# Address of one kind of weight parts in two tiles, and the grouping of 32 transposes, in a macaron layer

## Chip, cores, metric

One NeuronCore of a Trainium2 chip runs the whole kernel. The metric is the device time of one launch in microseconds; the profile is of one execution, and its span runs from the first to the last instruction.

## The reference

One layer on x of 512 tokens by 1024 channels, float32 throughout. What matters here is the feed-forward network (FFN), which is computed before and after a mixer:

```python
def swiglu_ffn(x, w_gate, w_up, w_down):
    return (jax.nn.silu(x @ w_gate) * (x @ w_up)) @ w_down

x = x + 0.5 * swiglu_ffn(rmsnorm(x, ffn1_norm[l]), ffn1_w_gate[l], ffn1_w_up[l], ffn1_w_down[l])
x = x + hybrid_mixer(rmsnorm(x, mix_norm[l]), ...)
x = x + 0.5 * swiglu_ffn(rmsnorm(x, ffn2_norm[l]), ffn2_w_gate[l], ffn2_w_up[l], ffn2_w_down[l])
x = rmsnorm(x, final_norm[l])
```

D_MODEL is 1024, D_FF is 2816, so `w_gate` and `w_up` have 22 tiles of 128 columns each. The mixer (attention over chunks and trailing means) is not touched by the change.

## The kernel before

**Products.** A float32 product is made of three float32r matmuls: each operand is split into a high part (`hi`, rounded to float32r) and a low part (`lo`, the rest), and `mm3` (lines 205 to 210) issues hi x hi (L208), hi x lo (L209) and lo x hi (L210) into one PSUM bank. ScalarE makes the high parts (a cast), VectorE the low ones (a subtraction). In the FFN's first half the weights are the stationary operand, which PE loads before each matmul, and the normalised x is the moving one.

**`ffn_up`** computes gate and up of one FFN (`loaded` is false in the first, true in the second). The 22 pairs of weight tiles are taken in two ways. The first `plain` = 5 pairs are multiplied directly: 8 row blocks of x, moving operand 512 tokens wide. The other 17 pairs, n = 5 to 21, go through a Strassen-like scheme with seven products of half size in place of eight: x's blocks are combined once into A11, A12, A22, S1 to S4, each 256 tokens wide, and per pair the weights' blocks are used as they are or added up. These are the half-size tiles. Each makes four sets of parts, `w[n, 11]` (W1), `w[n, 13]` (W1+W3 and a like sum), `w[n, 24]` (two longer sums) and `w[n, 22]` (helpers `high11` to `low24`, lines 520 to 580), and seven products of 12 matmuls of 256 columns, in this order: `w11` with A11; the second half of `w13` with S3; the first of `w24` with S2 and its second with A22; the first half of `w13` with S1; two with `w22`. So the second and the fifth product read the parts `w[n, 13]`.

**Where parts lie.** `part_tiles` hands out pairs of SBUF buffers of `ROOM` = 1152 elements in a cycle of four, so that each kind of parts always gets buffers of the same kind; `w[n, 13]` always gets the pair in the FFN's own pool. A part takes 1024 elements, from element `at` of its buffer: `AHEAD_OF_PARTS` = 16 for the half-size tiles. A buffer begins at 384 mod 512 bytes, so a part at element 16 begins at 448 mod 512 and one at element 32 (`OFF_AT`) at 0 mod 512. `high13` uses `OFF_AT` where `n - plain` is in `OFF`.

**The opening of the second FFN.** Here PE, VectorE and ScalarE run in the order in which the code is recorded. `OPENING` (line 63) writes it out by hand, token by token: `Wi` splits the i-th weight block into `w[i]` and fetches block i + 3; `B0` to `B3` multiply the first two pairs of tiles, two row blocks at a time, into the four banks `first` (24 triples of matmuls in all B1 to B3; `B3` is `last_block`); `P` and `L` are the tiles behind; `g`, `u`, `m` evacuate; `p` takes a piece of the work that combines x's blocks. B1 and B2 are `block(w, kp)` with kp 1 and 2: for each of two row blocks kk, four triples, one to each bank. Among these triples stand 32 transposes, `further`, one `by_token` each (line 1659): a 128x128 block of x, copied by DMA into the float32r tiles `xr` (rows 0 to 3 in the first, 4 to 7 in the second), is transposed on PE (L1666) into a PSUM bank of the four with tag "a". After every fourth one ScalarE copies the bank into a temporary (L1671) and SyncE's queue stores it to `x_d` in device memory (L1672), from where it is read again in the FFN's second half. The same queue issues the weight loads (L187, L522), in an order that a scheduler sets.

Of the kernel before, what the change touches and what calls it, by code (L numbers as in the profile page):

```python
# [21 lines left out]
NT = S // P  # L22
# [15 lines left out]


ROOM, AHEAD_OF_PARTS, ALIGN = 1024 + 128, 16, 64  # L40
OFF, OFF_AT = (0, 2, 6), 32
PLAIN = (5, 5)
RATES = [[2] * (n - 1) + [0] + [2] * (FF // P - n - 2) + [0] * 2 for n in PLAIN]
PROBS = 3
# [31 lines left out]
def layer(  # L76
# [51 lines left out]
    def temp(dtype=F32):  # L128
        return tpool.tile([P, S], dtype, tag="t", name=name("t"))

    def bank(tag="mm", bufs=4):
        return ps.tile([P, S], F32, tag=tag, name=name(tag), bufs=bufs)
# [52 lines left out]
    def raw_of(src):  # L185
        raw = raw_tile()
        nc.sync.dma_start(raw, src)  # L187
        return raw

    def parts_of(raw):  # L190
        hi, lo = part_tiles()
        split(raw, hi, lo)
        return hi, lo
# [11 lines left out]
    def mm3(acc, a, b, start, stop, further=False):  # L205

        more = dict(skip_group_check=True) if further else {}
        nc.tensor.matmul(acc, a[0], b[0], start=start, stop=False, **more)  # L208
        nc.tensor.matmul(acc, a[0], b[1], start=False, stop=False, **more)  # L209
        nc.tensor.matmul(acc, a[1], b[0], start=False, stop=stop, **more)  # L210

    def cut(pair, lo, n):
        if isinstance(pair[0], list):
            pair, lo = [z[lo // S] for z in pair], lo % S
        return pair[0][:, lo : lo + n], pair[1][:, lo : lo + n]
# [233 lines left out]
    def ffn_up(norm, wA, down, loaded, parts=(), aside=(), further=()):  # L449
# [24 lines left out]
        def block(w, kp):  # L474
            for kk in range(2):
                k = 2 * kp + kk
                for j in range(4):
                    mm3(first[j], cut(w, (kk * 4 + j) * P, P), norm.h[k], k == 0, k == KD - 1)
                    if kp:
                        for _ in range(min(1 + (j == 3), len(further))):  # L480
                            further.pop(0)()

        def nothing():
            pass
# [10 lines left out]
        def read_in():  # L495
            for kp in range(KD // 2):
                load(2 * kp)
                w = weights(wA[kp], 1 if kp else 4)
                load(2 * kp + 1)
                norm.square(2 * kp)  # L500
                norm.square(2 * kp + 1)
                if kp == KD // 2 - 1:
                    with tc.high_priority():
                        norm.finish(AF.Silu)
                block(w, kp)
            for f in range(2):
                sg = evacuate(f, *first[2 * f : 2 * f + 2])
                down.make_sums(sg, 2)
            blocks_of()
# [3 lines left out]
        def fetch(n, which):  # L513

            if n < KF:
                f = down.order[n]
                raw = raws[n, which] = down.pool.tile(
                    [P, 2 * S], F32, tag=which, name=name("raw"), bufs=RAW
                )
                half = slice(0, S) if which == "ra" else slice(S, 2 * S)  # L520
                for i, j in enumerate((1, 0) if which == "ra" else (0, 1)):
                    nc.sync.dma_start(raw[:, i * S : (i + 1) * S], wA[2 * f + j][:, half])  # L522
# [14 lines left out]
        def high11(n):  # L537
            if n < KF:
                high(n, (n, 11), raws[n, "ra"][:, :S])

        def low11(n):
            if n < KF:
                low((n, 11))

        def sum13(n):
            if n < KF:
                z = w[n, "odd"] = new_sum()
                a, b = raws[n, "ra"], raws[n, "rb"]
                nc.vector.tensor_tensor(z[:, :S], a[:, :S], a[:, S:], op=ALU.add)
                nc.vector.tensor_tensor(z[:, S:], a[:, S:], b[:, :S], op=ALU.add)  # L550

        def sum24(n):
            if n < KF:
                z = w[n, "even"] = new_sum()
                raw, odd = raws[n, "rb"], w[n, "odd"]
                nc.vector.tensor_tensor(z[:, :S], odd[:, :S], raw[:, :S], op=ALU.add)
                nc.vector.tensor_tensor(z[:, S:], z[:, :S], raw[:, S:], op=ALU.add)

        def high13(n):
            if n < KF:  # L560
                off = n - plain in OFF
                high(n, (n, 13), w[n, "odd"], OFF_AT if off else AHEAD_OF_PARTS)

        def low13(n):
            if n < KF:
                low((n, 13))

        def high24(n):
            if n < KF:
                high(n, (n, 24), w[n, "even"])  # L570

        def low24(n):
            if n < KF:
                low((n, 24))

        def opening():

            banks, halves_of = {f: first[2 * f : 2 * f + 2] for f in range(2)}, {}
            raw = dict(enumerate(parts[1:], 1))
            w = {0: parts[0]}  # L580
            steps = norm.steps()

            def fetch_raw(i):
                if i < 2 * plain and i not in raw:
                    raw[i] = raw_of(wA[i])

            def prepare(i):
                w[i] = parts_of(raw[i])
                fetch_raw(i + 3)

            def last_block():
                for j in range(4):
                    for kk in range(2):
                        k = KD - 2 + kk
                        mm3(first[j], cut(w[3], (kk * 4 + j) * P, P), norm.h[k], False, k == KD - 1)
                        for _ in range(min(1 + kk, len(further))):
                            further.pop(0)()

            def tile_product(n, j):
                acc = bank()  # L600
                banks.setdefault(n, []).append(acc)
                for k in range(KD):
                    mm3(acc, cut(w[2 * n + j], k * P, P), norm.h[k], k == 0, k == KD - 1)

            def last_tile(part):
                n = plain - 1
                if part == 0:
                    banks[n] = [bank(), bank()]
                for k in range(2 * part, 2 * part + 2):
                    for j in range(2):  # L610
                        mm3(
                            banks[n][j], cut(w[2 * n + j], k * P, P), norm.h[k], k == 0, k == KD - 1
                        )

            def gate(f):
                g, sg = temp(), temp()
                nc.vector.tensor_tensor(g, banks[f][0], norm.rb, op=ALU.mult)
                nc.scalar.activation(sg, g, AF.Silu)
                halves_of[f] = sg

            def up(f):
                sg = halves_of[f]
                nc.vector.tensor_tensor(sg, sg, norm.rb, op=ALU.mult)
                down.place(f, banks[f][1], sg)

            def sums(f):
                down.sums(f)
                down.make_sums(halves_of[f], 2)

            def half_size(what):  # L630
                n = plain
                if what == 0:
                    high11(n)
                    low11(n)
                elif what == 1:
                    sum13(n)
                elif what == 2:
                    high13(n)
                    low13(n)
                elif what == 3:  # L640
                    sum24(n)
                elif what == 4:
                    high24(n)
                else:
                    low24(n)

            def loads(what):
                fetch(plain + what // 2, ("ra", "rb")[what % 2])

            do = {  # L650
                "W": prepare, "B": lambda i: block(w[i], i) if i < 3 else last_block(),
                "P": lambda i: tile_product(i // 10, i % 10), "L": last_tile, "g": gate, "u": up,
                "m": sums, "h": half_size, "F": loads, "n": lambda i: next(steps), "p": piece,
                "O": lambda i: down.open(range(1, G - 3) if i else range(G - 3, G)),
            }
            for token in OPENING.split():
                do[token[0]](int(token[1:] or 1))
            assert not todo and not further
            return partial(up, plain - 1), partial(sums, plain - 1)
# [1241 lines left out]
```

## Time and profile before

| | |
|---|---|
| median of 3 runs | 837.81 us (837.65 to 838.47) |
| profiled execution | 838.23 us, span 836.5 us |
| PE busy | 826.8 us, 99% of the span |
| VectorE, ScalarE busy | 712.0 us (85%), 501.8 us (60%) |
| share of PE in the chain that ended last | 97% |
| half-size tiles | 62.4 to 224.7 us and 560.5 to 722.8 us |
| B1 to B3 of the second FFN | 507.8 to 527.8 us |

In PE's timeline a row's first number is the start of a matmul. Its length is modelled and overlaps the next one's, so what a matmul costs is read from one start to the next.

### The profile page before, as it was taken

The numbers are of one execution on the slowest core, as the hardware profiler recorded it, in microseconds if no ns is written. First come the engines' busy times: TensorE is split into PE (matmuls) and PEld (weight loads), VectorE is DVE, ScalarE is ACT, GpSimd is POOL, SyncE is SP. The second block draws the span as 40 slices with busy tenths as digits, with TensorE's granted clock in tenths as the row PEclk, the third lists the DMA queues.
The fourth block names the chain that finished last, engine by engine and source line by source line (L and its number), as shares of the span: only waits on it lengthen the run. The fifth ranks groups of instructions, "written<-read, shape, count | busy, mean of one in ns | idle before, by whom it ended". The sixth has DMA issues, their size and how long they took to land.

```text
span 836.5 us, 14350 instructions
## 1 busy us (share of the span) xinstructions
PE 826.8 (99%) x5288; PEld 740.3 (89%) x5288; DVE 712.0 (85%) x1157; ACT 501.8 (60%) x859; POOL 150.0 (18%) x212
## 2 busy tenths in 40 slices
PE   9999999999999999999999999999999999999996
PEld 7889999999988888887888887889999999988885
DVE  7999998899897678766979668989889999887896
ACT  8446555665675656558747745455566555756573
POOL 0312211222074000102111000111221121132600
PEclk9999999999999999999999999999999999999999
DMA  8667788888689973332221137757877888689922
GB/s 300 183 198 170 200 210 243 201 207 207 193 245 271 329 233 110 108 110 89 76 69 62 67 110 263 235 154 216 215 212 217 214 204 211 228 269 340 323 87 101
DMA packets 78839, 160.63 MB, mean 192 GB/s; under 512 B 7328, under 2 KB 30384, under 8 KB 78384
## 3 DMA queue, kind: packets, MB, share of 16 engines
q1 hardware_dynamic: 55680, 113.03, 40.1%
q0 software_dynamic: 22656, 46.14, 26.0%
q8 instruction: 41, 0.67, 0.3%
q10 hardware_dynamic: 432, 0.54, 0.2%
q14 instruction: 30, 0.25, 0.1%
HBM read 153.38 MB, written 50.34 MB: 244 GB/s over the span
## 4 chain that ended last, share of the span: by engine, by line
PE 97%; DMA 1%; DVE 1%; ACT 0%; SPq 0%; issue 0%; DVEq 0%
PE mm L208 23%; PE mm L210 23%; PE mm L209 23%; PE a L208 8%; PE a L209 8%; PE a L210 8%; PE a L1438 1%; PE a L1374 1%; PE a L1426 1%; DMA x<-in_xT_dram 1%; PE a L1296 0%; PE a L1666 0%; PE a L327 0%; PE a L1029 0%; PE mm L1029 0%; SPq L201 0%
## 5 line engine op out<-in xcount | busy, mean ns | idle before, releaser
L155 DVE TENSOR_TENSOR wlo<-raw,whi 128x1024 fp32r<-128x1024 f32 (+2 forms) x115 | 124.4, 1088 | 25.9 <-ACT whi L154 25.3
L154 ACT CAST whi<-raw 128x1024 fp32r<-128x1024 f32 (+2 forms) x115 | 107.3, 944 | 49.2 <-PE mm L210 13.0
L209 PE MATMUL mm<-ha,whi 128*128 128x256 f32 x408 | 112.8, 276 | 0.0
L208 PE MATMUL mm<-ha,whi 128*128 128x256 f32 x408 | 112.8, 276 | 0.0
L210 PE MATMUL mm<-ha,wlo 128*128 128x256 f32 x408 | 112.7, 276 | 0.0
L721 ACT ACTIVATE t<-mm 128x256 f32<-128x256 f32 x102 | 39.2, 384 | 114.3 <-PE mm L210 111.6
L531 DVE TENSOR_TENSOR wlo<-wsum,whi 128x1024 fp32r<-128x1024 f32 x68 | 83.0, 1220 | 11.0 <-PE mm L210 7.9
L866 POOL COPY mark<-t 128x1 f32<-128x1 f32 x44 | 14.3, 324 | 391.6 <-DVE t L774 243.0
L208 PE MATMUL mm<-hhi,whi 128*128 128x512 f32 x192 | 76.6, 401 | 0.9 <-ACT whi L154 0.6
L209 PEld LDWEIGHTS mm<-ha,whi 128*128 128x128 f32 x408 | 76.6, 188 | 0.1
L208 PEld LDWEIGHTS mm<-ha,whi 128*128 128x128 f32 x408 | 76.6, 188 | 0.1
L210 PEld LDWEIGHTS mm<-ha,wlo 128*128 128x128 f32 x408 | 76.6, 188 | 0.0
L209 PE MATMUL mm<-hlo,whi 128*128 128x512 f32 x192 | 74.9, 391 | 0.0
L210 PE MATMUL mm<-hhi,wlo 128*128 128x512 f32 x192 | 74.8, 391 | 0.0
L868 POOL DMA_DIRECT2D wsum<-in_wB_dram x72 | 71.1, 1102 | 12.3 <-issue 7.5
L526 ACT CAST whi<-wsum 128x1024 fp32r<-128x1024 f32 x68 | 67.9, 1047 | 2.0 <-PE mm L209 1.5
L209 PE MATMUL mm<-wlo,ah 128*128 128x512 f32 x176 | 68.5, 389 | 0.0
L210 PE MATMUL mm<-whi,ah 128*128 128x512 f32 x176 | 68.5, 389 | 0.0
L208 PE MATMUL mm<-whi,ah 128*128 128x512 f32 x176 | 68.4, 389 | 0.0
L531 DVE TENSOR_TENSOR wlo<-raw,whi 128x512 fp32r<-128x512 f32 x68 | 62.0, 950 | 0.0
L526 ACT CAST whi<-raw 128x512 fp32r<-128x512 f32 x68 | 56.2, 827 | 2.5 <-issue 2.5
L208 PE MATMUL a<-whi,ah 128*128 128x512 f32 (+1 forms) x154 | 55.7, 362 | 0.0
(233 smaller groups left out, 2398.7 us busy)
## 6 DMA issues: line engine op xcount, KB each, us to landing
raw<-in_wA_dram SPq DMA_DIRECT2D x136, 256.0 KB, 4.1
wsum<-in_wB_dram POOLq DMA_DIRECT2D x60, 512.0 KB, 6.9
raw<-wsum SPq DMA_DIRECT2D x40, 512.0 KB, 4.8
raw<-in_wB_dram SPq DMA_DIRECT2D x30, 512.0 KB, 7.4
wsum<-wsum POOLq DMA_DIRECT2D x20, 512.0 KB, 5.2
raw<-in_wA_dram SPq DMA_DIRECT2D x19, 512.0 KB, 4.1
x<-in_xT_dram SPq DMA_DIRECT2D x16, 256.0 KB, 8.8
raw<-in_wQK_dram SPq DMA_DIRECT2D x8, 512.0 KB, 3.5
```

The costliest lines, as they stand in the source:

```text
L154: nc.scalar.copy(hi, src)
L155: nc.vector.tensor_tensor(lo, src, hi.bitcast(F32), op=ALU.subtract)
L208: nc.tensor.matmul(acc, a[0], b[0], start=start, stop=False, **more)
L209: nc.tensor.matmul(acc, a[0], b[1], start=False, stop=False, **more)
L210: nc.tensor.matmul(acc, a[1], b[0], start=False, stop=stop, **more)
L526: nc.scalar.copy(hi, src)
L531: nc.vector.tensor_tensor(lo, src, hi.bitcast(F32), op=ALU.subtract)
L721: nc.scalar.activation(dst, src, AF.Copy, scale=scale)
L866: nc.gpsimd.tensor_copy(mark, after[:, 0:1])
L868: nc.gpsimd.dma_start(self.rows(i, g), self.rows(self.terms[i][at], g), **(dict(accum_op=ALU.add) if at else {}),)
L1374: nc.tensor.matmul(banks[i][:, at : at + n], qT[pair][0][a][rows, t * P : (t + 1) * P], kT[pair][0][b][rows, :n], start=a + b == 0, stop=a ...
L1426: nc.tensor.transpose(tp[:, n : n + P], prob[h, t][:, j * P : (j + 1) * P], ident)
```

## The change

`OFF` keeps its first entry alone, so that in the third and seventh half-size tile of both FFNs (n - plain = 2 and 6) W1+W3's parts begin at element 16 as in the others; the tiles' first entry keeps them at element 32. The transposes are no longer recorded behind each triple of B1, B2 and B3, but in runs of eight behind each of the two row blocks of B1 and of B2; B3 has none.

```diff
-OFF, OFF_AT = (0, 2, 6), 32
+OFF, OFF_AT = (0,), 32
...
                 for j in range(4):
                     mm3(first[j], cut(w, (kk * 4 + j) * P, P), norm.h[k], k == 0, k == KD - 1)
-                    if kp:
-                        for _ in range(min(1 + (j == 3), len(further))):
-                            further.pop(0)()
+                for _ in range(min(2 * NT if kp else 0, len(further))):
+                    further.pop(0)()
...
                         mm3(first[j], cut(w[3], (kk * 4 + j) * P, P), norm.h[k], False, k == KD - 1)
-                        for _ in range(min(1 + kk, len(further))):
-                            further.pop(0)()
```

The first edit moves no instruction, only addresses. The second moves instructions on PE, ScalarE and SyncE's queue; from L480 on, lines of the kernel after stand one to three lower in number.

PE at the end of B1's first row block, before. `mm_6068`, `mm_6069` and `mm_6066` are banks of `first`, `whi_6074` and `wlo_6075` are B1's weights, `a_6131` and `a_6148` the banks of the first and second four transposes:

```order
L210 MATMUL mm_6068<-hhi_5953,wlo_6075 128x512
L1666 MATMUL a_6131<-ident_r,xr_6049 128x128
L208 MATMUL mm_6069<-hhi_5953,whi_6074 128x512
L209 MATMUL mm_6069<-hlo_5954,whi_6074 128x512
L210 MATMUL mm_6069<-hhi_5953,wlo_6075 128x512
L1666 MATMUL a_6131<-ident_r,xr_6049 128x128
L1666 MATMUL a_6148<-ident_r,xr_6049 128x128
L208 MATMUL mm_6066<-hhi_5963,whi_6074 128x512
L209 MATMUL mm_6066<-hlo_5964,whi_6074 128x512
```

PE at the same place, after (`a_6140` and `a_6148` are the first two banks here):

```order
L208 MATMUL mm_6069<-hhi_5953,whi_6074 128x512
L209 MATMUL mm_6069<-hlo_5954,whi_6074 128x512
L210 MATMUL mm_6069<-hhi_5953,wlo_6075 128x512
L1663 MATMUL a_6140<-ident_r,xr_6049 128x128 x4
L1663 MATMUL a_6148<-ident_r,xr_6049 128x128 x4
L208 MATMUL mm_6066<-hhi_5963,whi_6074 128x512
L209 MATMUL mm_6066<-hlo_5964,whi_6074 128x512
L210 MATMUL mm_6066<-hhi_5963,wlo_6075 128x512
```

The transposes that stood singly behind each triple now follow one another in two groups of four, and the fourth triple of the row block follows the third directly.

ScalarE from the first copy out of a transposes' bank to the second SiLU, before. `whi_6171` is W3's high part (read in B3) and `whi_6229` W4's (read by P20); the rows L618 are the SiLU of the first two gates, the `a_` names are the banks of four transposes each:

```order
L1671 COPY t_6145<-a_6131 128x512
L1671 COPY t_6162<-a_6148 128x512
L154 CAST whi_6171<-raw_6056 128x1024
L1671 COPY t_6186<-a_6168 128x512
L1671 COPY t_6203<-a_6192 128x512
L1671 COPY t_6220<-a_6209 128x512
L154 CAST whi_6229<-raw_6078 128x1024
L1671 COPY t_6250<-a_6239 128x512
L1671 COPY t_6267<-a_6256 128x512
L1671 COPY t_6281<-a_6270 128x512
L618 ACTIVATE t_6285<-t_6284 128x512
L618 ACTIVATE t_6290<-t_6289 128x512
```

The same, after (`whi_6184` is W3's, `whi_6253` is W4's):

```order
L1668 COPY t_6145<-a_6140 128x512
L1668 COPY t_6153<-a_6148 128x512
L1668 COPY t_6173<-a_6168 128x512
L1668 COPY t_6181<-a_6176 128x512
L154 CAST whi_6184<-raw_6056 128x1024
L1668 COPY t_6208<-a_6203 128x512
L1668 COPY t_6216<-a_6211 128x512
L1668 COPY t_6236<-a_6231 128x512
L1668 COPY t_6244<-a_6239 128x512
L154 CAST whi_6253<-raw_6078 128x1024
L615 ACTIVATE t_6285<-t_6284 128x512
L615 ACTIVATE t_6290<-t_6289 128x512
```

Four copies now stand ahead of W3's cast where there were two, and eight ahead of W4's where there were five; none stands between W4's cast and the SiLU.

SyncE's queue, before: `x_d` rows are stores of transposed x, `raw_6233` is the load for W7, `raw_6175` that for W6, `raw_6482` the first loads of the half-size tiles:

```order
L1672 DMA x_d<-t_6145 128x512
L187 DMA raw_6233<-in_wA_dram 128x1024
L1672 DMA x_d<-t_6162 128x512
L187 DMA raw_6175<-in_wA_dram 128x1024
L1672 DMA x_d<-t_6186 128x512
L187 DMA raw_6327<-in_wA_dram 128x1024
L1672 DMA x_d<-t_6203 128x512
L522 DMA raw_6482<-in_wA_dram 128x512
L1672 DMA x_d<-t_6220 128x512
L522 DMA raw_6482<-in_wA_dram 128x512
```

After (`raw_6188` for W6, `raw_6257` for W7):

```order
L1669 DMA x_d<-t_6145 128x512
L1669 DMA x_d<-t_6153 128x512
L187 DMA raw_6188<-in_wA_dram 128x1024
L1669 DMA x_d<-t_6173 128x512
L1669 DMA x_d<-t_6181 128x512
L187 DMA raw_6257<-in_wA_dram 128x1024
L1669 DMA x_d<-t_6208 128x512
L1669 DMA x_d<-t_6216 128x512
L187 DMA raw_6327<-in_wA_dram 128x1024
L1669 DMA x_d<-t_6236 128x512
L1669 DMA x_d<-t_6244 128x512
L521 DMA raw_6482<-in_wA_dram 128x512 x2
```

W6's and W7's loads stand behind the second and the fourth store, where the first and the second of the two stood behind the first and the second store; the loads of the half-size tiles stand behind all eight.

## The prediction

> **What bounds the kernel now.** I read the page first: busy times, the granted clock, then the chain of work that ended last.
>
> ```profile
> span 836.5 us, 14350 instructions
> PE 826.8 (99%) x5288; PEld 740.3 (89%) x5288; DVE 712.0 (85%) x1157; ACT 501.8 (60%) x859; POOL 150.0 (18%) x212
> PEclk9999999999999999999999999999999999999999
> PE 97%; DMA 1%; DVE 1%; ACT 0%; SPq 0%; issue 0%; DVEq 0%
> L531 DVE TENSOR_TENSOR wlo<-wsum,whi 128x1024 fp32r<-128x1024 f32 x68 | 83.0, 1220 | 11.0 <-PE mm L210 7.9 <-ACT whi L526 2.7
> ```
>
> TensorE is the chain (97%), at the full granted clock throughout. VectorE, which makes the low parts of the weights, mostly waits for TensorE where it is idle ahead of the 1024-wide subtraction (7.9 of 11.0 us). So a change counts by what it does to the distances between starts of matmuls on PE, provided that no operand comes late. Both edits act there, and I read both from starts in PE's timeline.
>
> **The parts' place, third and seventh half-size tile.** A half-size tile is 7 products of 12 matmuls. Its second and fifth product load W1+W3's parts as the stationary operand; these are the only instructions on PE that the first edit touches. In the first FFN the third such tile starts at 81.64 and the fourth at 91.28. PE's timeline, with the first matmul of the first, second and third product of each:
>
> ```profile
> 81.64 0.28 PE L208 MATMUL mm<-ha,whi 128*128 128x256 f32 x1
> ...
> 83.00 0.28 PE L208 MATMUL a<-xa,whi 128*128 128x256 f32 x1
> ...
> 84.42 0.28 PE L208 MATMUL mm<-xa,whi 128*128 128x256 f32 x1
> ...
> 91.28 0.28 PE L208 MATMUL mm<-ha,whi 128*128 128x256 f32 x1
> ...
> 92.64 0.28 PE L208 MATMUL a<-xa,whi 128*128 128x256 f32 x1
> ...
> 94.00 0.28 PE L208 MATMUL mm<-xa,whi 128*128 128x256 f32 x1
> ```
>
> The second product takes 1.42 us in the third tile (parts at 0 mod 512 bytes), 1.36 us in the fourth (parts 64 bytes before such a place). The first product, whose parts are never moved, takes 1.36 us in both. Whole tiles, by windows from one tile's first matmul to the next (third, fourth, seventh, eighth; first FFN, then second):
>
> ```profile
> 81.64:91.28 9.64, 9.64 (x87) 1.00 0.81 247
> 91.28:100.80 9.52, 9.52 (x87) 1.00 0.82 210
> 119.84:129.48 9.64, 9.64 (x87) 1.00 1.03 217
> 129.48:139.00 9.52, 9.52 (x87) 1.00 0.90 224
> 579.73:589.37 9.64, 9.64 (x86) 1.00 0.82 265
> 589.37:598.89 9.52, 9.52 (x86) 1.00 0.79 208
> 617.93:627.57 9.64, 9.64 (x86) 1.00 0.98 218
> 627.57:637.09 9.52, 9.52 (x86) 1.00 0.81 221
> ```
>
> Four tiles are 0.12 us longer than their neighbours. With the parts at the ordinary place I take 9.52 us for them: 4 x 0.12 = **0.48 us saved**. Is VectorE ready for that? Its idle time waits for PE, so its work moves forward with PE. Zero is one bound (the tile would be slow for another reason); the other bound is a loss, the rival "slow pace" below.
>
> **The transposes.** 32 transposes of x, 128 columns each, stand among the 72 matmuls of 512 columns of B1, B2 and B3 in the second FFN. Before, one or two follow each group of three matmuls: 16 single, 8 pairs. After, eight follow each half of B1 and of B2, none stands in B3. PE's timeline around a single and a pair, then the last pair and the undisturbed matmuls behind it:
>
> ```profile
> 510.15 0.22 PE L1666 MATMUL a<-ident_r,xr 128*128 128x128 f32 x1
> 510.21 0.45 PE L208 MATMUL mm<-hhi,whi 128*128 128x512 f32 x1
> ...
> 510.96 0.28 PE L1666 MATMUL a<-ident_r,xr 128*128 128x128 f32 x2
> 511.08 0.46 PE L208 MATMUL mm<-hhi,whi 128*128 128x512 f32 x1
> ...
> 511.84 0.22 PE L1666 MATMUL a<-ident_r,xr 128*128 128x128 f32 x1
> ...
> 527.80 0.46 PE L208 MATMUL mm<-hhi,whi 128*128 128x512 f32 x1
> 528.10 0.39 PE L209 MATMUL mm<-hlo,whi 128*128 128x512 f32 x1
> ...
> 528.78 0.39 PE L209 MATMUL mm<-hlo,whi 128*128 128x512 f32 x1
> ```
>
> Three undisturbed matmuls take 0.68 us (528.10 to 528.78). With a single transpose the group takes 510.96 - 510.15 = 0.81, with a pair 511.84 - 510.96 = 0.88. So a single costs 0.13 us and the second of a pair 0.07. Over the whole stretch, from B1's first matmul at 507.84 to the first behind the last pair:
>
> ```profile
> 507.84:527.80 19.96, 19.96 (x106) 1.00 0.69 228
> ```
>
> 24 groups would take 24 x 0.68 = 16.32, so the transposes cost 19.96 - 16.32 = 3.64; the matmul at 527.80 holds the next back for 0.30 instead of 0.23, so 3.71 in all. With 24 x 0.13 = 3.12 for the first of each place, 8 seconds have 0.59, 0.07 each; rounding of 0.01 us in each start lets it be 0.07 to 0.09. I take 0.08. A run of eight then costs 0.13 + 7 x 0.08 = 0.69, and some 0.02 more because matmuls behind an interruption settle over more than the three that now follow. Four runs: 4 x 0.71 = 2.84. **Saved: 3.71 - 2.84 = 0.87 us.**
>
> The price of the third to eighth transpose of a run is not in the trace. Below it lies 0.06 (the two starts of the pair at 510.96 are followed by the next matmul's at 511.08): a run then costs 0.57, four 2.28, saved 1.43. Above it lies the kernel's longest run of transposes, ten of plain float32 in the mixer:
>
> ```profile
> 422.03 1.25 PE L1426 MATMUL a<-ident,prob 128*128 128x128 f32 x10
> 423.04 0.48 PE L208 MATMUL mm<-hhi,whi 128*128 128x512 f32 x1
> 423.35 0.40 PE L209 MATMUL mm<-hlo,whi 128*128 128x512 f32 x1
> ```
>
> From 422.03 to 423.35 are ten transposes and one matmul of 0.23: 1.09, or 0.11 each. By that a run of eight costs 0.13 + 7 x 0.11 + 0.02 = 0.92, four 3.68: saved 0.03. I take 0.08, since the pair is the same instruction on the same tiles. A loss would need PE to wait inside or before a run. A run fills two of the four "a" banks, and ScalarE empties a bank in 0.59 us (below) while 12 matmuls, 2.7 us, lie between runs; xr is there, for the first run needs the same four transposes by 511 as before, and the third starts at 507.84 + 36 x 0.227 + 2 x 0.71 = 517.4, 12 us behind the issue of the last xr load (505.07 in SyncE's rows):
>
> ```profile
> 505.07 0.55 SPq L1657 DMA_DIRECT2D xr<-x  x1
> 514.21 1.05 ACT L154 CAST whi<-raw 128x1024 fp32r<-128x1024 f32 x1
> 521.21 0.59 ACT L1671 COPY t<-a 128x512 f32<-128x512 f32 x1 [1.90 <-PE a L1666]
> 521.69 1.05 ACT L154 CAST whi<-raw 128x1024 fp32r<-128x1024 f32 x1
> 522.77 1.23 DVE L155 TENSOR_TENSOR wlo<-raw,whi 128x1024 fp32r<-128x1024 f32 x1 [1.10 <-ACT whi L154]
> 524.58 0.68 DVE L617 TENSOR_TENSOR t<-mm,rb 128x512 f32<-128x512 f32 x1
> 529.14 0.69 DVE L623 TENSOR_TENSOR t<-t,rb 128x512 f32<-128x512 f32 x1 [1.02 <-ACT t L618]
> ```
>
> What is queued behind: on ScalarE W3's cast (514.21 before) and W4's (521.69 before) now stand behind four copies each. B1 ends at 507.84 + 5.44 + 1.42 = 514.7, its last two copies at 515.5, W3's cast at 516.5, its low part on VectorE at 517.7; B3, which needs it, starts at 521.6. W4: last copies 522.4, cast 523.4, low part 524.6, then gate 0 (524.58 before) at about 525.3 to 526.0, which frees the bank that P20 writes; P20 starts at 521.6 + 5.44 = 527.0. The smallest margin is thus 1.0 us. Behind that VectorE gains: its wait of 1.02 us at 529.14, for a SiLU that stood behind B3's last copy, goes. On SyncE two weight loads (W6, W7) now stand behind the second and fourth store of x, at about 512.4 and 515.6; their casts are the second and third behind 529.5, over 10 us later. I cost all of this at nothing; if gate 0 came 1 us later still, P20 would wait for it.
>
> *A rule against it.* By the Trainium skill, "TensorE: Matmul & The Clock Gate", section "LDWEIGHTS (loading the stationary operand)", a load of 128 columns takes 128 / 1.2 = 107 ns, and behind a matmul of 128 columns it cannot hide. The trace agrees for the float32 run (0.11 each) and not for the second of a float32r pair (0.08). By the page a run would cost 0.13 + 7 x 0.107 + 0.02 = 0.90, the four 3.60, and the edit would save 0.11 instead of 0.87.
>
> **The sum.** The profiled execution took 838.23 us (span 836.5). 838.23 - 0.48 - 0.87 = 836.88. It stands 0.42 above the median of the runs, 837.81; the forecast against that median is 837.81 - 1.35 = **836.5 us**, 0.16% faster. A measurement of this kernel can tell about 0.2%, 1.68 us, from no change.
>
> **The rivals.**
>
> *Every transpose of a run pays a full weight load (0.11 us).* For it speaks the float32 run, against it the pair. Total saved 0.48 + 0.03 = 0.51: 837.3 us.
>
> *Transposes in a long run go at 0.06.* For it speak the starts inside the pair, against it that the next matmul is held to 0.30 behind them, as if the debt were only shown later. Saved 0.48 + 1.43 = 1.91: 835.9 us, over the bound.
>
> *Slow pace, ending slower.* The first product of the first half-size tile has its parts at the ordinary place and still runs slowly:
>
> ```profile
> 62.42 0.28 PE L208 MATMUL mm<-ha,whi 128*128 128x256 f32 x1
> ...
> 63.84 0.28 PE L208 MATMUL a<-xa,whi 128*128 128x256 f32 x1
> ```
>
> 1.42 us, not 1.36. So there is a slow pace that does not come from the address, and here it ended with the moved parts of that tile. If these parts are what brings PE back to 1.36, then taking them from the third and seventh tile leaves PE without that should the slow pace return. Slow, a tile takes 7 x 0.06 = 0.42 longer; from the third tile to the seventeenth that is 15 x 0.42 = 6.3 us in one FFN: 836.5 + 6.3 + 0.24 (the saving there, lost) = 843.0 us. It is slower by over 0.2% from (1.68 + 1.35) / 0.42, some 7 slow tiles. Against it: the first product of the third tile, ahead of the moved parts, was at 1.36, and the fourth and eighth tiles, which lack them, took 9.52.
>
> *Nothing gained from the place.* The tile would then still take 9.64, and 0.87 alone is saved: 836.9 us. Against it: the excess sits in the products that load these parts.
>
> **How the numbers follow.** Forecast 0.55; full weight load in a run 0.19; 0.06 in a run 0.12; slow pace 0.10; nothing from the place 0.04. The runs of before reach from 0.16 below to 0.66 above the median, so a case near a bound can fall on either side: of the forecast's 0.55 I put 0.10 beyond 0.2% faster (its seconds at 0.07 would save 0.28 more: 1.63) and 0.02 beyond 0.2% slower. Faster 0.12 + 0.10 = 0.22, slower 0.10 + 0.02 = 0.12, same 0.66. The range goes from the 0.06 case less 0.2 of scatter, 835.7, to the full weight load plus 0.6 of scatter, 837.9; outside it are the slow pace and the tails.
>
> **What would show it.** In the profile after: windows of 9.52 us for the third and seventh tile, of both FFNs; second products of 1.36. PE's timeline from B1's first matmul to P20's first: 16.32 + 4 x 0.71 = 19.2 us, from 19.96; inside a run, the time from the first transpose to the second matmul behind it, less 0.23, is 8 transposes' cost: 0.71 is mine, 0.92 the full load's, 0.57 the fast run's. VectorE's wait ahead of L623 is gone, and P20 starts without a wait. I am wrong if products with parts at the ordinary place take 1.42 behind the first tile, or if PE waits at B3 or P20.

## The result: 0.16% faster, with the profile after

The kernel after takes 836.88 us (median of 20 runs, 836.33 to 839.13), the kernel before in the same rounds 838.12. The ratio is 0.9984, with a 95% interval of 0.9978 to 0.9991. One of the 20 runs before took 1187.22 us and is no part of the ratio. The medians lie 1.24 us apart, where 1.35 was forecast; the time itself is 0.4 us above the forecast of 836.5, mostly because the median before is 0.31 above the one that the forecast started from. The profiled execution has a span of 835.3 us, 1.2 less than before.

The page after: total, busy times, the granted clock, the chain.

```profile
span 835.3 us, 14350 instructions
PE 826.3 (99%) x5288; PEld 741.2 (89%) x5288; DVE 711.3 (85%) x1157; ACT 501.1 (60%) x859; POOL 149.8 (18%) x212
PEclk9999999999999999999999999999999999999999
PE 98%; DMA 1%; DVE 1%; SPq 0%; ACT 0%; issue 0%; DVEq 0%
```

PE is still the chain. Windows of the third and seventh half-size tile of both FFNs, each from its first matmul to the next tile's first, then of the stretch from B1's first matmul to P20's first (bounds, length, PE busy and instructions, granted clock, DMA share and GB/s), and last, for comparison with the experiments, of the first FFN's first half-size tile:

```profile
81.27:90.79 9.52, 9.52 (x86) 1.00 0.79 252
119.35:128.87 9.52, 9.52 (x86) 1.00 1.03 212
578.68:588.20 9.52, 9.52 (x86) 1.00 0.83 271
616.76:626.28 9.52, 9.52 (x86) 1.00 0.96 220
507.54:526.82 19.28, 19.28 (x105) 1.00 0.74 246
62.05:71.75 9.70, 9.70 (x85) 1.00 0.33 110
```

All four tiles are at 9.52, from 9.64. The stretch took 19.96 before, and the matmul at its end held the next one back by another 0.07, which does not happen now; the second edit saves 0.68 to 0.75 us. PE's timeline at the first run of eight:

```profile
510.26 0.80 PE L1663 MATMUL a<-ident_r,xr 128*128 128x128 f32 x8
510.90 0.46 PE L208 MATMUL mm<-hhi,whi 128*128 128x512 f32 x1
511.20 0.40 PE L209 MATMUL mm<-hlo,whi 128*128 128x512 f32 x1
```

From the first transpose to the second matmul behind the run are 0.94 us; less 0.23 for one matmul, the run costs 0.71 us, 0.089 for each transpose.

The two terms give 0.48 + 0.7 = 1.2 us, as the span has it. That the spans agree so well is partly luck. Between the two profiles the first half-size tile also begins 0.37 us earlier (62.42 and 62.05), and 0.31 of that is lost between the first FFN's last half-size tile and B1 (224.68 to 507.84 and 224.07 to 507.54). The first is not an effect of the edits: in the ten profiles below, whose code is the same ahead of the half-size tiles but for addresses, that beginning lies between 61.48 and 62.71. The second holds a late operand. PE and its weight loads (PEld) after, in the first FFN's second half:

```profile
282.67 0.39 PE L208 MATMUL a<-whi,ah 128*128 128x512 f32 x1
282.99 0.19 PEld L209 LDWEIGHTS a<-wlo,ah 128*128 128x128 f32 x1 [0.35 <-DVE wlo L155]
282.99 0.51 PE L209 MATMUL a<-wlo,ah 128*128 128x512 f32 x1
```

PE waits for a low part here, and 0.32 us lie between two starts where 0.23 is usual. From the last half-size tile's end to B1 the kernel before takes 283.16 us and this one 283.47; the five profiles below whose third and seventh tiles are at 9.52 take 283.13 to 283.51. So part of a gain ahead of this place is lost in some executions and not in others.

### The profile page after: what moved, and what is told of

Read it like the earlier page. It is cut to its first block, busy times and chain, and to the rows that moved or that the text cites. A ratio compares the mean times of both kernels' runs of the same rounds, so it can differ in the third digit from the quotient of the medians.

```text
span 835.3 us, 14350 instructions
## 1 busy us (share of the span) xinstructions
PE 826.3 (99%) x5288; PEld 741.2 (89%) x5288; DVE 711.3 (85%) x1157; ACT 501.1 (60%) x859; POOL 149.8 (18%) x212
## 4 chain that ended last, share of the span: by engine, by line
PE 98%; DMA 1%; DVE 1%; SPq 0%; ACT 0%; issue 0%; DVEq 0%
PE mm L208 23%; PE mm L210 23%; PE mm L209 23%; PE a L209 8%; PE a L210 8%; PE a L208 8%; PE a L1435 1%; PE a L1371 1%; PE a L1423 1%; DMA raw<-in_wA_dram 1%; PE a L1293 0%; PE a L1663 0%; PE mm L1026 0%; PE a L1026 0%; PE a L327 0%; SPq L201 0%
```

## Experiments

Ratios are to the kernel before, run in the same rounds.

**Each edit alone.** The kernel before with the first edit:

```diff
-OFF, OFF_AT = (0, 2, 6), 32
+OFF, OFF_AT = (0,), 32
```

> The kernel before with the first edit alone: W1+W3's parts of the third and seventh half-size tile at the ordinary place. Theory (the address alone sets the pace): these four tiles take 9.52 us instead of 9.64, 0.48 us in all; PE's stretch of B1 to B3 stays at 19.96 us. In the first FFN a part of its 0.24 us may be lost at a wait for weights near 283 us, where the profile after shows PE held up; so the time falls by 0.24 to 0.48 us, ratio 0.9994 to 0.9997. Rival (slow pace returns without these parts): tiles of 9.9 us behind the second, 1.5 to 12 us slower.

Ratio 0.9996 (0.9988 to 1.0005). Windows of its third and seventh tile and of B1 to P20:

```profile
81.36:90.88 9.52, 9.52 (x86) 1.00 0.82 247
119.44:128.96 9.52, 9.52 (x86) 1.00 1.07 220
507.44:527.37 19.93, 19.93 (x105) 1.00 0.68 228
```

The tiles are 9.52 and the stretch is what it was, within 0.03. The time itself does not tell 0.48 us from nothing. Next the second edit alone, made from the kernel after:

```diff
-OFF, OFF_AT = (0,), 32
+OFF, OFF_AT = (0, 2, 6), 32
```

> The kernel after with the third and seventh tile's parts back at 0 mod 512, so that the runs of eight transposes alone are left of the change. Theory (each further transpose of a run costs one load of its operand, 0.085 us): B1's first matmul to P20's first 19.29 us as after, from 19.96; 0.74 us saved, ratio 0.9991. The third and seventh tiles take 9.64 us again. Rival (the edits help each other, PE's timing behind the runs matters in the tiles): tiles of another length than 9.64, or a saving under 0.4 us.

Ratio 0.9991 (0.9982 to 1.0000), as expected. Its third and seventh tile and the stretch:

```profile
81.46:91.10 9.64, 9.64 (x87) 1.00 0.79 240
119.54:129.18 9.64, 9.64 (x86) 1.00 1.06 219
507.65:526.97 19.32, 19.32 (x105) 1.00 0.72 240
```

The third and seventh tile are back at 9.64. So the edits do not touch each other, and 0.9996 x 0.9991 = 0.9987 agrees with 0.9984 within the intervals. This profile has a span of 837.4 us, longer than before although its terms are shorter. PE's timeline in the second FFN's second half (the bracket is the wait and what ended it):

```profile
759.79 0.39 PE L210 MATMUL mm<-whi,ah 128*128 128x512 f32 x1
760.70 0.49 PE L208 MATMUL mm<-whi,ah 128*128 128x512 f32 x1 [0.51 <-ACT whi L154]
761.95 0.50 PE L209 MATMUL mm<-wlo,ah 128*128 128x512 f32 x1 [0.76 <-DVE wlo L155]
```

and ScalarE's, with what it waited for:

```profile
759.60 1.57 ACT L154 CAST whi<-raw 128x1024 fp32r<-128x1024 f32 x2 [4.59 <-DMA raw<-wsum]
```

A load of summed weights landed late and held PE up by 1.7 us (starts at 759.79, 760.70 and 761.95, where 0.23 lies between undisturbed ones). In the kernel after, the low part that the second of these matmuls reads is ready only 0.06 us ahead of it, worked out from the end of VectorE's subtraction. The profile with T3 and T4 shifted shows the same loss of 1.7 us; those with no moved part and with moved parts in every tile show smaller ones, 1.04 and 0.31 us lost between two starts, in the first FFN's second half. That single runs lie 1.7 us and more above their median may come from such loads; for runs without a profile it is not shown.

**Do the moved parts matter at all?** No part at 0 mod 512, not even in the first tile:

```diff
-OFF, OFF_AT = (0,), 32
+OFF, OFF_AT = (), 32
```

> The kernel after with no part at 0 mod 512, not even in the first half-size tile. Rival of the prediction (moved parts end the slow pace in which the first tile begins): without them the first product's pace of 0.118 us per matmul goes on, tiles of about 9.9 us, for some or all of the 17 tiles of an FFN, 0.4 us for each, up to 13 us slower. Theory (the address sets the pace, the slow beginning is a transient of some matmuls): the first tile takes 9.52 to 9.6 us instead of 9.70, all others 9.52, 0.2 to 0.35 us faster than after.

1.0136 (1.0122 to 1.0149), 849.6 us. Windows of the first, second, sixteenth and seventeenth tile of the first FFN:

```profile
61.48:71.37 9.89, 9.89 (x85) 1.00 0.32 108
71.37:81.27 9.90, 9.90 (x87) 1.00 1.05 216
209.87:219.77 9.90, 9.90 (x86) 1.00 0.98 208
219.77:229.66 9.89, 9.89 (x86) 1.00 0.52 162
```

All 34 tiles take 9.89: the pace at which the first product of the stage runs, 0.118 us per matmul, goes on to its end. From 9.52, and from 9.70 in the first tile of each FFN, that is 32 x 0.37 + 2 x 0.19 = 12.2 us. The theory that the address alone sets the pace fell; the rival stands. Next, the moved parts in the fifth tile instead of the first:

```diff
-OFF, OFF_AT = (0,), 32
+OFF, OFF_AT = (4,), 32
```

> The kernel after with W1+W3's parts at 0 mod 512 in the fifth half-size tile instead of the first. Theory (the slow pace keeps itself up until such a product ends it): the first four tiles take 9.89 us, the fifth about 9.75, all behind it 9.52; slower than after by 4 x 0.37 - 0.18 + 0.2, about 1.5 us in each FFN, 3 us in all. Rival (what counts is the beginning of the stage): 9.89 throughout, 12.8 us slower than after.

One run, 839.43 us. The fourth, fifth, sixth and seventeenth tile:

```profile
91.47:101.36 9.89, 9.89 (x86) 1.00 0.78 196
101.36:111.06 9.70, 9.70 (x86) 1.00 0.97 244
111.06:120.58 9.52, 9.52 (x86) 1.00 0.50 168
215.78:225.30 9.52, 9.52 (x86) 1.00 0.53 171
```

Four slow tiles, one that turns, and 9.52 to the end. The second FFN shows the same numbers. So products with their parts at 0 mod 512 end the slow pace in the fifth tile as in the first, and one tile of them is enough for all that follow. Whether another place than 0 would end it as well was not tried.

**The address.** Moved parts in every tile of the kernel after:

```diff
-OFF, OFF_AT = (0,), 32
+OFF, OFF_AT = range(17), 32
```

> The kernel after with W1+W3's parts at 0 mod 512 in all 17 half-size tiles of both FFNs. Theory (address): every tile from the second on takes 9.64 us, 32 tiles by 0.12 = 3.8 us slower than after, ratio to before about 1.003. Rival (the excess of the third and seventh tile belongs to those tiles and not to the address): 9.52 in the others, no change.

1.0030 (1.0018 to 1.0042). The second and the seventeenth tile:

```profile
71.74:81.38 9.64, 9.64 (x87) 1.00 1.00 206
216.34:225.98 9.64, 9.64 (x87) 1.00 0.53 168
```

0.12 us in every tile behind the first, as in the third and seventh of before: the price belongs to the address. Now all parts at 384 mod 512, where the moving operand lies too (the first tile's moved ones stay at 0):

```diff
-ROOM, AHEAD_OF_PARTS, ALIGN = 1024 + 128, 16, 64
+ROOM, AHEAD_OF_PARTS, ALIGN = 1024 + 128, 0, 64
```

> The kernel after with all parts of the half-size tiles at 384 mod 512 bytes, as the moving operand is (the first tile's moved ones stay at 0). Theory A (the pace depends on how the stationary operand's address stands to the moving one's): both at 384, as in the last products of the second FFN's second half, where 256 columns take 0.119 us per matmul; so about 0.119 instead of 0.113 in all half-size tiles, 10.0 us a tile, 34 tiles by 0.45 = 15 us slower than after. Theory B (only 0 mod 512 is slow): no change.

1.0203 (1.0188 to 1.0219), the first and second tile:

```profile
61.73:71.75 10.02, 10.02 (x85) 1.00 0.33 106
71.75:81.83 10.08, 10.08 (x86) 1.00 1.04 216
```

10.08 is 0.120 us per matmul, and the moved parts of the first tile end nothing here. Theory B, that only 0 mod 512 is slow, fell. Theory A, that it depends on how the two addresses stand to each other, fits; but only the weights were moved, so a rule by the weights' own address fits as well. In the second half of the second FFN, 132 of the 198 matmuls of the products T3 and T4 are 256 columns wide, with both operands at 384; there the moving one was shifted:

```diff
-            hi, lo = part_tiles()
+            hi, lo = part_tiles(AHEAD_OF_PARTS if self.wide and i in (T3, T4) else 0)
```

(`self.wide` is true in the second FFN alone.)

> The kernel after, with the weight parts of the products T3 and T4 of the second FFN's second half (there the moving operand; half of their matmuls are 256 columns wide) at 448 mod 512 instead of 384. Theory A (how the two addresses stand to each other sets the pace): the 131 matmuls of 256 columns take 0.113 us instead of 0.119, 0.7 to 0.85 us faster than after. Theory B (the stationary operand alone matters, or only 0 mod 512): no change from after.

0.9986 (0.9977 to 0.9994), no different from after. The first 102 of these matmuls stand in groups of six between matmuls of 512 columns, the last 30 in one row; that row from its first start to its last, 29 distances, in the kernel after and here:

```profile
823.89:827.36 3.47, 3.47 (x30) 1.00 0.21 86
825.50:828.92 3.42, 3.42 (x30) 1.00 0.21 84
```

They take 0.118 us, the slow pace, instead of 0.120; over all of them the mean falls from 0.119 to 0.118. Theory A's 0.113 did not come, but nothing here lies at 0 mod 512 to end a slow pace. So the shift alone is not enough, and which rule sets the pace stays open.

**The transposes.** Plain float32 in the same places:

```diff
-                tp[:, j * P : (j + 1) * P].bitcast(F32R), xr[half][:, j, t * P : (t + 1) * P], ident_r
+                tp[:, j * P : (j + 1) * P], xr[half][:, j, t * P : (t + 1) * P].bitcast(F32), ident
```

> The kernel after, its 32 transposes on plain float32 operands instead of float32r, in the same places. Theory (a run costs a load of its stationary operand for each transpose, and a float32 transpose takes 0.109 us in the mixer's runs): a run of eight costs 8 x 0.109 + 0.03 = 0.90 us instead of 0.74, B1 to P20 19.9 us instead of 19.29, 0.65 us slower than after, as before. Rival (the type does not matter; in the mixer something else holds the transposes): 19.29 us as after.

0.9995 (0.9986 to 1.0004). B1 to P20, and the first run in PE's timeline:

```profile
507.18:527.08 19.90, 19.90 (x105) 1.00 0.73 249
```

```profile
509.92 1.03 PE L1663 MATMUL a<-ident,xr 128*128 128x128 f32 x8
510.70 0.48 PE L208 MATMUL mm<-hhi,whi 128*128 128x512 f32 x1
511.02 0.40 PE L209 MATMUL mm<-hlo,whi 128*128 128x512 f32 x1
```

509.92 to 511.02 less 0.23 is 0.87, 0.109 for each: the price of the mixer's float32 runs. With it the stretch gains 0.06 to 0.13 us on the kernel before, instead of 0.68 to 0.75. The type sets the price. Now two runs of sixteen:

```diff
-                for _ in range(min(2 * NT if kp else 0, len(further))):
+                for _ in range(min(4 * NT if kp and kk else 0, len(further))):
```

> The kernel after with two runs of sixteen transposes, at the end of B1 and of B2, instead of four of eight. Theory (a run costs 0.03 plus 0.085 a transpose, and settling of some 0.05 behind it): two interruptions less save 2 x 0.07 = 0.14 us, B1 to P20 about 19.15 us. Rival (PE waits for one of the four banks, or W3's low part comes late, as four copies stand ahead of its cast at B1's end): 19.3 us or more.

0.9984 (0.9976 to 0.9993):

```profile
507.20:526.38 19.18, 19.18 (x105) 1.00 0.72 250
```

0.10 us less in the stretch than with four runs; in time it cannot be told from after.

**A version meant to beat both**: two runs of sixteen, and W1's parts at 0 mod 512 in the first tile in place of W1+W3's.

```diff
-                high(n, (n, 11), raws[n, "ra"][:, :S])
+                high(n, (n, 11), raws[n, "ra"][:, :S], OFF_AT if n - plain in OFF else AHEAD_OF_PARTS)
...
-                high(n, (n, 13), w[n, "odd"], OFF_AT if off else AHEAD_OF_PARTS)
+                high(n, (n, 13), w[n, "odd"])
```

> A version meant to beat both: two runs of sixteen transposes, and in the first half-size tile W1's parts at 0 mod 512 in place of W1+W3's (W1's serve one product, W1+W3's two). Theory (any product with parts there ends the slow pace, which otherwise goes on): first product 1.42 us as ever, the other six 1.36, so the first tile takes 9.58 us instead of 9.70, the others 9.52; with 0.10 us from the runs 0.34 us faster than after, ratio to before about 0.998. Rival (one product is not enough, or it must not be the one that follows the 512-wide matmuls): tiles of 9.89 us throughout, 13 us slower than after.

0.9985 (0.9976 to 0.9994). The first and second tile and the stretch:

```profile
62.71:72.32 9.61, 9.61 (x85) 1.00 0.33 111
72.32:81.84 9.52, 9.52 (x86) 1.00 0.98 200
507.77:526.95 19.18, 19.18 (x106) 1.00 0.73 249
```

One product is enough to end the slow pace. The first tile is 0.09 us shorter in each FFN, the stretch 0.10; the 0.28 us in sum are seen in the trace and not in the time, whose runs reach from 835.64 to 837.90.

## Why the prediction was right, step by step

*The parts' place*: right, 4 x 0.12 us, shown by the profiles with the first edit alone, with the second alone and with the moved parts in all tiles.

*The transposes*: right in the mechanism, 0.75 us with what was owed behind the stretch, instead of 0.87. The mis-sized term is the 2.84 us for the four runs: the stretch less its 72 matmuls is 19.28 - 16.32 = 2.96. A run is 0.71 by the starts, as forecast, but the matmuls behind it settle for 0.03 us more per run, which I had put inside the 0.71.

*Full weight load in a run*: fell for float32r (0.089), holds for float32 (0.109). By the Trainium skill, "TensorE: Matmul & The Clock Gate", section "LDWEIGHTS (loading the stationary operand)", a load takes its columns divided by 1.2 in ns, which gives an estimate of 107 ns for 128 columns; the trace agrees for float32 (109 ns) and not for float32r (89 ns). The 0.06 case fell too: only the first two distances of a run are that short (0.059 and 0.065 us in the run above), the next ones are 0.08 to 0.09.

*Nothing queued behind comes late*: right at the places that were checked. VectorE's rows around gate 0 after, and behind it:

```profile
525.00 0.68 DVE L614 TENSOR_TENSOR t<-mm,rb 128x512 f32<-128x512 f32 x1
525.60 1.22 DVE L409 TENSOR_TENSOR aside<-aside,aside 128x1024 f32<-128x1024 f32 x1
...
528.46 0.69 DVE L620 TENSOR_TENSOR t<-t,rb 128x512 f32<-128x512 f32 x1
```

Gate 0 ends at 525.7, 1.1 us ahead of P20 at 526.8 (forecast: 1.0), and the wait of 1.02 us ahead of the third row is gone. What I did not look for lies elsewhere: in the FFNs' second halves weights can arrive with margins as small as 0.06 us, or late, so a gain of PE ahead of them can be lost there, as at 282.99 in the profile after. That the spans still differ by the sum of the terms is the luck named above.

*Slow pace*: it did not happen, but the mechanism is real and reaches farther than I had priced. A slow tile costs 0.37 us, not 0.42, and without any moved part all 34 are slow. What I held against it, tiles at the fast pace that lack moved parts, holds; the runs add that the first tile's parts, which the change leaves, are what ends the slow pace for all tiles behind. Why the third and seventh had moved parts before is open; no run here shows the slow pace coming back without them. What in the chip keeps up either pace is open too.

## What to carry to other kernels

Where TensorE is the bound, read the distance between starts product by product: two regular paces of the same instruction are a hint at addresses or at a state that keeps itself up. Before removing an odd setting, ask which of its instances does the work, and try none and a late one as well. Short transposes among long matmuls cost most where each stands alone: 0.13 us for a single one before, 0.089 for each of eight in a row. What a row costs depends on the type: as plain float32 each took 0.109, and such rows gained almost nothing on single float32r ones.

## What the runs showed of the hardware

- With the weights at 448 and the moving operand at 384 mod 512 bytes (places by the program's layout), float32r matmuls of 256 columns have two lasting paces, 0.113 and 0.118 us (9.52 and 9.89 for a tile of 84). The stage enters at 0.118 behind matmuls of 512 columns and stayed there for 17 tiles (1428 matmuls); 12 matmuls whose weights lie at 0 mod 512 led to 0.113, which then lasted to the stage's end, 16 tiles and more.
- With both operands at 384 mod 512 the pace is 0.120 (10.08 for a tile), and products with weights at 0 did not end it.
- A float32r transpose of 128x128 costs 0.089 us in a run of eight among matmuls of 512 columns, a float32 one 0.109.
